# A program order for ACT and DVE in an attention stage, a second PSUM bank for its filler projections, paired statistics, and two start-up steps dealt otherwise

## The chip, the cores and the metric

The kernel runs on one core of a Trainium2 chip. The metric is the device time of one execution, in microseconds (us). The core's engines are TensorE (PE, its weight loads shown as PEld), VectorE (DVE), ScalarE (ACT), GpSimd (POOL) and SyncE (SP, which here issues nearly all DMAs). Each takes its instructions in one fixed order, and they meet through semaphores.

## The reference

One step of a hybrid encoder with one mixer layer, 1024 prompt frames and 32 running frames, width 1024, 16 heads of 64. Both branches read one normalized input:

```python
h = rmsnorm(x, norm_g)
q, k = rmsnorm(h @ Wq, q_g) * 64**-0.5, rmsnorm(h @ Wk, k_g)    # per head
v, logf = h @ Wv, log_sigmoid(h @ Wf + b_f)
ga, gb, ma, mb = h @ Wga, h @ Wgb, h @ Wma, h @ Wmb
u = (h @ Wua) * sigmoid(h @ Wub)
o = causal_softmax_attention(q, k, v, bias = C[t] - C[s])       # C = cumsum(logf)
conv = causal_depthwise_conv(u, w_dw, width 31) + b_dw
ya = (o * silu(ga)) @ w_pa
yb = (silu(layernorm(conv)) * silu(gb)) @ w_pb
y = x + (sigmoid(ma) * ya + sigmoid(mb) * yb) @ w_out
```

The 32 running frames attend to 512 cached keys besides their own. Outputs are y, k, v, logf and the last convolution rows, all fp32.

## The kernel before

**Products.** For accuracy each operand is split into a high and a low part. A product is three matmuls (high by high, low by high, high by low). In the input projections the parts are fp16; in the attention and behind it they are fp32 rows. A projection of 128 output channels is three chunks of 352 frames, each of eight steps of three matmuls (`steps`, `mms` at L183). Each step of three calls `beat`: a tick, the clock of the program. Small jobs hang on ticks: `later(n, fn)` emits work n ticks on, `prep` holds the preparation of the next weights, and `taps` and `chores` are DVE work (convolution taps at L368, above all) dealt out at a fixed rate per tick.

**Weights.** A batch is two keys (or one half-width value key). In `begin`, the batch now starting emits: `load` of the following batch at ticks 5 and 15, `stage` (a sum of squares on ACT, L117, with a small POOL cast, L120) at 3 and 13, `total` (a PE sum across partitions) at 25, `power` at 27, and `split` (ACT writes the high part, L138, DVE the low part, L141) from 29 on. A batch of two keys lasts 48 ticks. So a load is issued in one batch, and its squares are taken in the next.

**Stages in order of time.** The opening transposes and splits x in three column groups (`x_split`) while it makes the first two projections (`high(i, p)` and `low(i, p)` split slice p of their weights, `known(i)` finds their scale, `rooted` takes the roots of the rows' squares, `squares(t)` the squares of row block t). Then come the values (L760), the convolution inputs u, keys and queries (`qk`), the gate ga, the attention, and the output products.

**Keys and queries.** ACT squares each chunk (L865) and writes the high part (L866), POOL the low part `sql` (L869), PE sums over heads with two fp32 matmuls into a bank of `st` (L876, L877), ACT forms the inverse root (L879, L880), and DVE scales the chunk out of PSUM (L883). The chunk's PSUM bank, one of five, is held until then. The statistics come 11 ticks behind the square, chunk by chunk.

**Attention.** The sequence `seq` holds 16 heads of 8 blocks and four `Sample` items for the running frames. `start(seq[n + 3])` makes the scores of the block three places ahead: PE into one of two buffers of psS (two banks each), DVE adds the mask (L1097) and takes the maximum (L1099), ACT the exponential P (L1102), DVE a reciprocal (L1104), POOL scales P (L1105). `turn` transposes block n on PE (L1119) into banks of psT, from which ACT copies the first four parts and DVE the rest (L1122). `values`, once a head, multiplies the transposed P with V (L1138) into two psT banks; ACT and DVE add them into ot (L1142, L1143, L1145). Between these PE gets `fill`: ticks of 22 gate projections of no urgency, each chunk in the single bank of the pool `pq`, copied out by ACT (L932). PE and SP run in the order of the program there; the order of ACT, DVE and POOL is found by a scheduler that simulates time. In the stages before the attention PE, DVE and ACT are all in program order.

```python
    pe.enter_context(tc.manual_schedule(engines={E.PE, E.SP}))
    ...
    psS = pool("psS", 2, stack=p2, space=PS)
    psT = pool("psT", 3, stack=p2, space=PS)
```

The eight PSUM banks of the attention are thus four of psS, three of psT and one of pq.

Of the kernel before, what the change touches and what calls it, by code (L numbers as in the profile page):

```python
# [53 lines left out]
def build(tc, xT, xt, wv, wf, ckT, cv, clT, stT, vec, cst, yT, kT, vO, lfO, cpT, csT):  # L54
# [166 lines left out]
    def begin():  # L221

        if not plan:
            return
        b = plan.pop(0)
        after = plan[0] if plan else None
        t = pace["tick"]
        jobs = [(25, b.total), (27, b.power)]
        if b.n == 2:
            jobs += [(3, lambda: b.stage(0)), (13, lambda: b.stage(1))]  # L230
            for i, n in ((0, 29), (1, 39)):
                jobs.append((n, lambda i=i: b.split(i)))
                jobs += [(n + 1 + 2 * p, lambda i=i, p=p: b.rest(i, p)) for p in range(3)]
        else:
            jobs += [(3 + 10 * i, lambda i=i: b.stage(i)) for i in range(2)]
            jobs.append((29, lambda: split.__setitem__(b.keys[0], split_v(b.keys[0][1], b))))
        if after:
            jobs += [(5 + 10 * i, after.load) for i in range(after.n)]
        prep.extend((t + n, fn) for n, fn in sorted(jobs, key=lambda e: e[0]))
# [377 lines left out]
    scale(1, 1, True)  # L617
    scale(0, 1)
    known(0)
    high(0, 0)  # L620
    low(0, 0)
    steps_of = {}

    def rooted(t0, nt):
        steps_of[t0] = root(t0, nt)
# [12 lines left out]
    for f in range(8):  # L638
# [12 lines left out]
    b1 = plan.pop(0)  # L651
    b2 = plan[0]
    x_split(0, ws0, u0, {
        0: [lambda: top(1), lambda: squares(2, False)],
        1: [lambda: squares(3)],
        2: [lambda: high(0, 1), lambda: low(0, 1)],
        3: [lambda: total(2), lambda: squares(4, False)],
        4: [lambda: known(1), lambda: rooted(2, 3), lambda: high(1, 0), lambda: low(1, 0), lambda: high(0, 2)],
        5: [lambda: steps_of[2](), lambda: scale(2, 0), lambda: scale(3, 0, True), lambda: scale(4, 0), lambda: low(0, 2)],
        6: [lambda: scale(3, 1, True), lambda: scale(2, 1), lambda: high(1, 1), lambda: low(1, 1)],  # L660
        7: [lambda: scale(4, 1), lambda: high(1, 2), lambda: low(1, 2)]})
# [189 lines left out]

    pqk = ExitStack()
    tp = pool("tp", 2, stack=pqk, side="right")
    def qk(g, f):
        gv, dst, smp = (vec_t[:, V_KG:V_KG + 1], s_k, ks_t) if g == "k" else (qg8, s_q, qs_t)
        qn = tp.tile([128, TT], F32, name="qn", tag="qn")
        gi = tp.tile([128, 1], F32, name="gi", tag="gi")

        def ev(c, sl, ps, inv):
            if c == 0:  # L860
                nc.gpsimd.tensor_scalar(gi, inv, gv, 1.0, op0=ALU.mult, op1=ALU.mult)
            sqf = tp.tile([128, CH], F32, name="sqf", tag="sqf")
            sqh = tp.tile([128, CH], F32R, name="sqh", tag="sqh", bufs=3)
            sql = tp.tile([128, CH], F32R, name="sql", tag="sql", bufs=3)
            nc.scalar.activation(sqf, ps, AF.Square, scale=inv)  # L865
            nc.scalar.copy(sqh, sqf)  # L866

            def low():
                nc.gpsimd.tensor_sub(sql, sqf, f32(sqh))  # L869

            later(2, low)
            later(11, lambda: root(c, sl, ps, sqh, sql))

        def root(c, sl, ps, sqh, sql):
            pm = st.tile([128, 512], F32, name="pst", tag="st")
            nc.tensor.matmul(pm[:, :CH], bones, sqh, start=True, stop=False)  # L876
            nc.tensor.matmul(pm[:, :CH], bones, sql, start=False, stop=True)  # L877
            ri = tp.tile([128, CH], F32, name="ri", tag="ri")
            nc.scalar.activation(ri, pm[:, :CH], AF.Ln, bias=eps_t, scale=1.0 / HD)  # L879
            nc.scalar.activation(ri, ri, AF.Exp, scale=-0.5)  # L880

            def scaled():
                nc.vector.scalar_tensor_tensor(qn[:, sl], ps, gi, ri, op0=ALU.mult, op1=ALU.mult)  # L883
                later(6, lambda: out(c))

            later(4, scaled)

        def out(c):
            n = CH if c < 2 else T - 2 * CH
            o = slice(c * CH, c * CH + n)  # L890
            qh = tp.tile([128, CH], F32R, name="qh", tag="qh")
            ql = tp.tile([128, CH], F32R, name="ql", tag="ql")
            nc.scalar.copy(qh[:, :n], qn[:, o])  # L893
            nc.gpsimd.tensor_sub(ql[:, :n], qn[:, o], f32(qh[:, :n]))  # L894
            nc.sync.dma_start(dst[0, f * 128:(f + 1) * 128, o], f32(qh[:, :n]))
            nc.sync.dma_start(dst[1, f * 128:(f + 1) * 128, o], f32(ql[:, :n]))
            if c == 2:
                if g == "k":
                    nc.sync.dma_start(kT[f], qn)
                nc.gpsimd.tensor_scalar(smp[:, f, :], qn[:, T:TT], 1.0, 1.0, op0=ALU.mult, op1=ALU.mult)  # L900

        proj((g, f), X, XL, pj, ev)
# [80 lines left out]


    pe = ExitStack()
    pe.enter_context(tc.manual_schedule(engines={E.PE, E.SP}))
    pace["rate"], pace["credit"] = R_A, 0.0
    taps.extend(sums(7))
    psS = pool("psS", 2, stack=p2, space=PS)
    psT = pool("psT", 3, stack=p2, space=PS)  # L990
    totals.append((psT, "T"))
    ap = pool("ap", 2, stack=p2, side="right")

    def filler():

        for n in range(NFILL):
            yield from gate_steps(*fills.pop(0), pq)

    flow = filler()

# [4 lines left out]
    class Sample:  # L1005
# [15 lines left out]
        def scores(self):  # L1021
            g, kc, pf = self.g, self.kc, self.pf
            ps = psS.tile([128, 2, 512], F32, name="psS", tag="S")
            for j in range(4):
                rows = slice(64 * (j % 2), 64 * (j % 2) + 64)
                q = qs_t[rows, 2 * g + j // 2, :]
                nc.tensor.matmul(ps[32 * j:32 * j + 32, 0, :], q, kc[rows, j // 2, :], start=True, stop=True)
                nc.tensor.matmul(ps[32 * j:32 * j + 32, 1, :TS], q, ks_t[rows, 2 * g + j // 2, :],
                                 start=True, stop=True)
            nc.vector.scalar_tensor_tensor(pf[:, :PAST], ps[:, 0, :], cq[:, g:g + 1], pf[:, :PAST],  # L1030
                                           op0=ALU.add, op1=ALU.subtract)
            nc.vector.scalar_tensor_tensor(pf[:, PAST:], ps[:, 1, :TS], cq[:, g:g + 1], pf[:, PAST:],
                                           op0=ALU.add, op1=ALU.subtract)
            nc.vector.tensor_add(pf[:, PAST:], pf[:, PAST:], smask)
            nm = ap.tile([128, 3], F32, name="nm", tag="nm", bufs=6)
            nc.vector.tensor_reduce(nm[:, 0:1], pf, axis=AX.X, op=ALU.max, negate=True)
            nc.scalar.activation(pf, pf, AF.Exp, bias=nm[:, 0:1], accum_out=nm[:, 1:2])
            nc.vector.reciprocal(nm[:, 2:3], nm[:, 1:2])
            nc.vector.tensor_scalar(pf, pf, nm[:, 2:3], None, op0=ALU.mult)

# [36 lines left out]
    class Block:  # L1077
# [5 lines left out]
        def scores(self):  # L1083
# [13 lines left out]
            nc.vector.tensor_add(diag, diag, cmask)  # L1097
            nm = ap.tile([128, 3], F32, name="nm", tag="nm", bufs=6)
            nc.vector.tensor_reduce(nm[:, 0:1], ps[:, :nb, :w], axis=AX.XY, op=ALU.max, negate=True)  # L1099
            self.P = P = ap.tile([128, T], F32, name="P", tag="P", bufs=3)  # L1100
            with tc.issue_after(sides["tables"].ins):
                nc.scalar.activation(P[:, :nk].rearrange("p (b w) -> p b w", b=nb), ps[:, :nb, :w], AF.Exp,  # L1102
                                     bias=nm[:, 0:1], accum_out=nm[:, 1:2])
            nc.vector.reciprocal(nm[:, 2:3], nm[:, 1:2])  # L1104
            nc.gpsimd.tensor_scalar(P[:, :nk], P[:, :nk], nm[:, 2:3], 1.0, op0=ALU.mult, op1=ALU.mult)  # L1105

# [94 lines left out]
    sides["shift"] = ap.tile([128, TT], F32, name="shift", bufs=1)  # L1201
    nc.sync.dma_start(sides["shift"], s_m)
    heads[1].load()
    start(seq[0])
    fill(8)
    start(seq[1])
    fill(4)
    start(seq[2])
    for n, b in enumerate(seq):
        if n + 3 < len(seq):  # L1210
            start(seq[n + 3])
        if n + 9 < len(seq) and getattr(seq[n + 9], "i", 1) == 0:
            seq[n + 9].head.load()
        if n + 6 < len(seq) and isinstance(seq[n + 6], Sample):
            seq[n + 6].load()
        if getattr(b, "i", 0) == 3 and b.head.h + 1 < H:
            heads[b.head.h + 1].load_v()
        if isinstance(b, Sample):
            fill(4)
            b.turn()  # L1220
        else:
            b.turn()
            fill(4 if b.i > 2 or b.head.h != 8 else 0)
        if n >= 2 and pending(seq[n - 2]):
            seq[n - 2].values()
        if n >= 3 and isinstance(seq[n - 3], Sample):
            seq[n - 3].finish()
        if "ready" in sides:
            next(ln, None)
# [402 lines left out]
```

## Time and profile before

| | |
|---|---|
| median of three runs | 1370.6 us (1367.92 to 1372.93) |
| profiled execution | 1370.8 us |
| its span, first to last instruction | 1368.9 us |
| mean granted clock of TensorE | 0.993 |
| busy share of PE, DVE, ACT, POOL | 97%, 71%, 53%, 37% |

The profile is of one execution. "Busy" of an engine is the time in which one of its instructions ran. Matmuls overlap in the array, so PE is shown busy for longer than it takes to issue them. The profile notes for each instruction how long its engine had been idle before it and what released it; a wait for several things is put down to the one that came last. The "chain" follows the work back from the last instruction through what released each step.

### The profile page before, as it was taken

Reading aid. Unit: us, or ns where it says so; the run is one execution under the profiler, and the core shown is the slowest. Engines: PE = TensorE matmul, PEld = TensorE weight load, DVE = VectorE, ACT = ScalarE, POOL = GpSimd, SP = SyncE. Lnnn points to the kernel's source line nnn. Section 1 sums busy time; section 2 is a strip of 40 time slices with the busy share of each in tenths; the row PEclk is TensorE's granted clock in tenths of the full one; section 3 lists DMA queues with packets and bytes.
Section 4 is the critical chain, followed back from the end, with each engine's and each line's share of the span. In section 5 each row is a group of like instructions: output and inputs, shape, how many; then the busy total and the mean of one; then the engine's idle time right before and its main releaser. Section 6 shows DMA issues by size and latency. Waiting matters only on the chain.

```text
span 1368.9 us, 24793 instructions
## 1 busy us (share of the span) xinstructions
PE 1321.6 (97%) x9383; PEld 1004.6 (73%) x9383; DVE 976.6 (71%) x1534; ACT 721.7 (53%) x1360; POOL 500.2 (37%) x548
## 2 busy tenths in 40 slices
PE   8999999999999999989999899999999999999999
PEld 5577876666666666666667667667666699999998
DVE  6787879778888897978778756644454479266664
ACT  6544555757676743555545556655555466333320
POOL 2001125547475820244323232222222239355553
PEclk9999999999999999999999999999999999999999
DMA  6233233425252453544634644455542597634462
GB/s 246 96 129 109 91 111 120 132 88 176 94 172 78 172 160 110 162 106 130 168 108 125 173 124 123 130 158 126 144 118 80 177 327 261 212 114 141 145 194 68
DMA packets 113495, 194.96 MB, mean 142 GB/s; under 512 B 34080, under 2 KB 80032, under 8 KB 113376
## 3 DMA queue, kind: packets, MB, share of 16 engines
q1 hardware_dynamic: 113232, 193.31, 46.2%
q8 instruction: 74, 1.21, 0.4%
q14 instruction: 45, 0.37, 0.1%
q10 hardware_dynamic: 144, 0.07, 0.0%
HBM read 127.68 MB, written 65.64 MB: 141 GB/s over the span
## 4 chain that ended last, share of the span: by engine, by line
PE 73%; DVE 8%; DMA 6%; ACT 6%; issue 4%; SPq 1%; POOL 1%; ACTq 0%; DVEq 0%; POOLq 0%
PE pj L183 51%; PE pjv L760 6%; PE pj L1464 5%; DMA raw<-wf 4%; PE po L1138 3%; PE ptr L1119 2%; DVE y L368 2%; DVE nm L1099 2%; ACT P L1102 2%; PE psS L1094 1%; PE psS L1095 1%; DVE wl L141 1%; ACT t L932 1%; ACT junk L117 1%; DMA a<-s_o 1%
## 5 line engine op out<-in xcount | busy, mean ns | idle before, releaser
L183 PE MATMUL pj<-xh,wh 128*128 128x352 f16 (+2 forms) x1536 | 483.8, 315 | 20.9 <-ACT t L932 17.1
L183 PE MATMUL pj<-xh,wl 128*128 128x352 f16 (+2 forms) x1536 | 483.3, 315 | 0.4 <-DVE wl L141 0.4
L183 PE MATMUL pj<-xl,wh 128*128 128x352 f16 (+2 forms) x1536 | 483.2, 315 | 0.4 <-DVE xl L576 0.2
L183 PEld LDWEIGHTS <-wh 128*128 128x128 f16 x3072 | 302.2, 98 | 164.0 <-ACT wh L138 3.6
L368 DVE SCALAR_TENSOR_TENSOR y<-u,vec_t,y 128x1086 f32<-128x1086 f32 x240 | 343.7, 1433 | 9.5 <-ACT y L365 6.6
L1105 POOL TENSOR_SCALAR P<-P,nm 128x128 f32<-128x128 f32 (+7 forms) x128 | 122.1, 955 | 281.0 <-DVE nm L1104 231.2
L183 PEld LDWEIGHTS <-wl 128*128 128x128 f16 x1536 | 151.1, 98 | 93.7 <-issue 22.4
L141 DVE SCALAR_TENSOR_TENSOR wl<-raw,sc,wh 128x384 f16<-128x384 f32 (+1 forms) x192 | 120.8, 663 | 31.5 <-ACT wh L138 31.5
L1102 ACT ACTIVATE P<-psS,nm 128x128 f32<-128x128 f32 (+7 forms) x128 | 94.7, 740 | 77.9 <-DVE nm L1099 64.1
L1099 DVE TENSOR_REDUCE nm<-psS 128x1 f32<-128x128 f32 (+7 forms) x128 | 96.2, 754 | 7.1 <-DVE psS L1097 0.5
L1122 ACT COPY pt<-ptr 128x512 f32<-128x512 f32 (+3 forms) x128 | 64.2, 502 | 59.9 <-PE ptr L1119 59.0
L175 POOL TENSOR_TENSOR wl<-raw,wh 128x384 fp32r<-128x384 f32 (+1 forms) x51 | 63.3, 1268 | 75.0 <-ACT wh L172 57.8
L1094 PE MATMUL psS<-KB,QB 128*128 128x256 f32 (+2 forms) x192 | 81.9, 428 | 9.0 <-ACT P L1102 8.9
L117 ACT ACTIVATE junk<-raw 128x1024 bf16<-128x1024 f32 x62 | 65.2, 1052 | 37.8 <-DMA raw<-wf 37.7
L1119 PE MATMUL ptr<-ident,P 128*128 128x128 f32 x576 | 85.0, 274 | 0.0
L869 POOL TENSOR_TENSOR sql<-sqf,sqh 128x352 fp32r<-128x352 f32 x48 | 59.4, 1238 | 49.9 <-ACT sqh L866 49.8
L138 ACT ACTIVATE wh<-raw,sc 128x1024 f16<-128x1024 f32 (+1 forms) x68 | 72.6, 1089 | 6.8 <-DVE sc L158 6.6
L1119 PEld LDWEIGHTS ptr<-ident,P 128*128 128x128 f32 x576 | 69.8, 142 | 5.7 <-ACT pt L1122 0.2
L1138 PE MATMUL po<-pt,V 128*64 128x256 f32 x640 | 72.6, 382 | 0.0
L120 POOL CAST topb<-tops 128x2 bf16<-128x2 f32 x35 | 12.9, 367 | 162.8 <-ACT junk L117 112.8
L894 POOL TENSOR_TENSOR ql<-qn,qh 128x352 fp32r<-128x352 f32 (+1 forms) x48 | 62.8, 1311 | 22.2 <-ACT qh L893 22.2
L1097 DVE TENSOR_TENSOR psS<-psS,cmask 128x128 f32<-128x128 f32 x128 | 37.5, 294 | 46.8 <-PE psS L1095 46.2
(271 smaller groups left out, 2601.9 us busy)
## 6 DMA issues: line engine op xcount, KB each, us to landing
raw<-wf SPq DMA_DIRECT2D x92, 512.0 KB
QB<-s_q SPq DMA_DIRECT2D x32, 256.0 KB
KB<-s_k SPq DMA_DIRECT2D x32, 256.0 KB
kT<-qn SPq DMA_DIRECT2D x8, 528.0 KB
s_ga<-t SPq DMA_DIRECT2D x24, 176.0 KB
s_gb<-t SPq DMA_DIRECT2D x24, 176.0 KB
s_ma<-t SPq DMA_DIRECT2D x24, 176.0 KB
s_mb<-t SPq DMA_DIRECT2D x24, 176.0 KB
```

The costliest lines, as they stand in the source:

```text
L117: nc.scalar.activation(junk[:, :raw.shape[1] * raw.shape[2]], raw.rearrange("p a b -> p (a b)"), AF.Square, accum_out=self.tops[:, i:i + 1])
L138: nc.scalar.mul(wh[:, ks, :], raw[:, ks, :], self.s[:, i:i + 1])
L141: nc.vector.scalar_tensor_tensor(wl[:, ks, :], raw[:, ks, :], self.s[:, i:i + 1], wh[:, ks, :], op0=ALU.mult, op1=ALU.subtract)
L183: nc.tensor.matmul(ps, a[:, kt, :], b(kt, sl), start=(first and n == 0), stop=(last and n == N - 1))
L368: t = nc.vector.scalar_tensor_tensor(y, u[:, i:i + CW], w, y, op0=ALU.mult, op1=ALU.add)
L760: nc.tensor.matmul(ps[:, :VC], a, b, start=(n == 0), stop=(n == 23))
L1094: nc.tensor.matmul(ps[:, b, :wm], QB[:, qsl], KB[:, ksl], start=True, stop=False)
L1099: nc.vector.tensor_reduce(nm[:, 0:1], ps[:, :nb, :w], axis=AX.XY, op=ALU.max, negate=True)
L1102: nc.scalar.activation(P[:, :nk].rearrange("p (b w) -> p b w", b=nb), ps[:, :nb, :w], AF.Exp, bias=nm[:, 0:1], accum_out=nm[:, 1:2])
L1105: nc.gpsimd.tensor_scalar(P[:, :nk], P[:, :nk], nm[:, 2:3], 1.0, op0=ALU.mult, op1=ALU.mult)
L1119: nc.tensor.transpose(pt[:, 128 * j:128 * j + 128], P[:, 128 * (4 * u + j):128 * (4 * u + j) + 128], ident)
L1138: nc.tensor.matmul(po[rows], V[:, j, :], parts[c][:, j, :], start=(c % 2 == 0 and j < 2), stop=(c % 2 == 1 and j >= 2 * c))
```

## The change

- Attention: DVE and ACT join PE and SP in program order. psT has two banks for three, and the freed bank becomes a second pool `pq2`; the fills' chunks take `pq` and `pq2` in turn.
- The blocks' and samples' `scores` are cut in three: scores up to the maximum, `soft` (the exponential) and `norm` (reciprocal and scaling). In step n they are emitted as: scores of n+3, turn of n, soft of n+3, norm of n+2. The fill of four ticks is cut in two halves with the values between them.
- Keys and queries: the statistics of two chunks are made together, 13 ticks behind the second one's square; sqh and sql have four buffers for three.
- First value weights: stage at ticks 10 and 17 (from 3 and 13), total at 32 (from 25), power at 33 (from 27), split at 34 (from 29).
- Opening: the first slice of the first split moves behind the first transposes; `known(1)` and `squares(4)`, the latter from DVE to ACT, change places; the second split's first slice goes ahead of the roots.

```diff
         jobs = [(25, b.total), (27, b.power)]
-        if b.n == 2:
+        if b.keys[0] == ("v", 0):
+            jobs = [(32, b.total), (33, b.power), (10, lambda: b.stage(0)), (17, lambda: b.stage(1)),
+                    (34, lambda: split.__setitem__(b.keys[0], split_v(0, b)))]
+        elif b.n == 2:
...
     known(0)
-    high(0, 0)
-    low(0, 0)
...
     x_split(0, ws0, u0, {
-        0: [lambda: top(1), lambda: squares(2, False)],
+        0: [lambda: high(0, 0), lambda: low(0, 0), lambda: top(1), lambda: squares(2, False)],
...
-        3: [lambda: total(2), lambda: squares(4, False)],
-        4: [lambda: known(1), lambda: rooted(2, 3), lambda: high(1, 0), lambda: low(1, 0), lambda: high(0, 2)],
+        3: [lambda: total(2), lambda: known(1), lambda: squares(4)],
+        4: [lambda: high(1, 0), lambda: low(1, 0), lambda: rooted(2, 3), lambda: high(0, 2)],
...
+    duo = []
+
+    def stats(both):
+        pms = [st.tile([128, 512], F32, name="pst", tag="st") for _ in both]
+        for pm, (_, sqh, sql) in zip(pms, both):
+            nc.tensor.matmul(pm[:, :CH], bones, sqh, start=True, stop=False)
+            nc.tensor.matmul(pm[:, :CH], bones, sql, start=False, stop=True)
+        for i, (pm, (fn, _, _)) in enumerate(zip(pms, both)):
+            later(i, lambda pm=pm, fn=fn: fn(pm))
...
             later(2, low)
-            later(11, lambda: root(c, sl, ps, sqh, sql))
+            duo.append((lambda pm: root(c, sl, ps, pm), sqh, sql))
+            if len(duo) == 2:
+                both = list(duo)
+                duo.clear()
+                later(13, lambda: stats(both))
...
-    pe.enter_context(tc.manual_schedule(engines={E.PE, E.SP}))
+    pe.enter_context(tc.manual_schedule(engines={E.PE, E.SP, E.DVE, E.Activation}))
...
-    psT = pool("psT", 3, stack=p2, space=PS)
+    psT = pool("psT", 2, stack=p2, space=PS)
+    pq2 = pool("pq2", 1, stack=p2, space=PS)
...
+    class Two:
+        n = 0
+
+        def tile(self, *a, **k):
+            self.n += 1
+            return (pq2 if self.n % 2 else pq).tile(*a, **k)
...
-            yield from gate_steps(*fills.pop(0), pq)
+            yield from gate_steps(*fills.pop(0), two)
...
             nc.vector.tensor_reduce(nm[:, 0:1], ps[:, :nb, :w], axis=AX.XY, op=ALU.max, negate=True)
+            self.at = ps, nm, nk, nb, w
+
+        def soft(self):
+            ps, nm, nk, nb, w = self.at
             self.P = P = ap.tile([128, T], F32, name="P", tag="P", bufs=3)
...
+        def norm(self):
+            P, nm, nk = self.P, *self.at[1:3]
             nc.vector.reciprocal(nm[:, 2:3], nm[:, 1:2])
...
-        if isinstance(b, Sample):
-            fill(4)
-            b.turn()
-        else:
-            b.turn()
-            fill(4 if b.i > 2 or b.head.h != 8 else 0)
+        b.turn()
+        if n + 3 < len(seq):
+            seq[n + 3].soft()
+        if n + 2 < len(seq):
+            seq[n + 2].norm()
+        some = 2 if isinstance(b, Sample) or b.i > 2 or b.head.h != 8 else 0
+        fill(some)
         if n >= 2 and pending(seq[n - 2]):
             seq[n - 2].values()
+        fill(some)
```

More of the change, by code (lines that the diff above doesn't have):

```diff
@@ L862, in ev @@
             sqf = tp.tile([128, CH], F32, name="sqf", tag="sqf")
-            sqh = tp.tile([128, CH], F32R, name="sqh", tag="sqh", bufs=3)
-            sql = tp.tile([128, CH], F32R, name="sql", tag="sql", bufs=3)
+            sqh = tp.tile([128, CH], F32R, name="sqh", tag="sqh", bufs=4)
+            sql = tp.tile([128, CH], F32R, name="sql", tag="sql", bufs=4)
             nc.scalar.activation(sqf, ps, AF.Square, scale=inv)
@@ L871, in ev, with root @@
             later(2, low)
-            later(11, lambda: root(c, sl, ps, sqh, sql))
[L874 to L877, printed above, removed]
+            duo.append((lambda pm: root(c, sl, ps, pm), sqh, sql))
[3 more added lines that the diff above has]
+                later(13, lambda: stats(both))
+        def root(c, sl, ps, pm):
             ri = tp.tile([128, CH], F32, name="ri", tag="ri")
@@ L989, in build @@
     psS = pool("psS", 2, stack=p2, space=PS)
-    psT = pool("psT", 3, stack=p2, space=PS)
+    psT = pool("psT", 2, stack=p2, space=PS)
+    pq2 = pool("pq2", 1, stack=p2, space=PS)
     totals.append((psT, "T"))
     ap = pool("ap", 2, stack=p2, side="right")
+    class Two:
[3 more added lines that the diff above has]
+            return (pq2 if self.n % 2 else pq).tile(*a, **k)
+    two = Two()
     def filler():
         for n in range(NFILL):
-            yield from gate_steps(*fills.pop(0), pq)
+            yield from gate_steps(*fills.pop(0), two)
     flow = filler()
@@ L1034, in scores @@
             nc.vector.tensor_add(pf[:, PAST:], pf[:, PAST:], smask)
-            nm = ap.tile([128, 3], F32, name="nm", tag="nm", bufs=6)
+            self.nm = nm = ap.tile([128, 3], F32, name="nm", tag="nm", bufs=6)
             nc.vector.tensor_reduce(nm[:, 0:1], pf, axis=AX.X, op=ALU.max, negate=True)
-            nc.scalar.activation(pf, pf, AF.Exp, bias=nm[:, 0:1], accum_out=nm[:, 1:2])
+        def soft(self):
+            nc.scalar.activation(self.pf, self.pf, AF.Exp, bias=self.nm[:, 0:1], accum_out=self.nm[:, 1:2])
+        def norm(self):
+            nm, pf = self.nm, self.pf
             nc.vector.reciprocal(nm[:, 2:3], nm[:, 1:2])
@@ L1099, in scores, with soft @@
             nc.vector.tensor_reduce(nm[:, 0:1], ps[:, :nb, :w], axis=AX.XY, op=ALU.max, negate=True)
+            self.at = ps, nm, nk, nb, w
+        def soft(self):
+            ps, nm, nk, nb, w = self.at
             self.P = P = ap.tile([128, T], F32, name="P", tag="P", bufs=3)
@@ L1103, in scores, with norm @@
                                      bias=nm[:, 0:1], accum_out=nm[:, 1:2])
+        def norm(self):
+            P, nm, nk = self.P, *self.at[1:3]
             nc.vector.reciprocal(nm[:, 2:3], nm[:, 1:2])
@@ L1203, in build @@
     heads[1].load()
-    start(seq[0])
-    fill(8)
-    start(seq[1])
-    fill(4)
-    start(seq[2])
+    for n in range(3):
+        start(seq[n])
+        seq[n].soft()
+        if n:
+            seq[n - 1].norm()
+        fill((8, 4, 0)[n])
     for n, b in enumerate(seq):
@@ L1217, in build @@
             heads[b.head.h + 1].load_v()
-        if isinstance(b, Sample):
-            fill(4)
-            b.turn()
-        else:
-            b.turn()
-            fill(4 if b.i > 2 or b.head.h != 8 else 0)
+        b.turn()
[5 more added lines that the diff above has]
+        fill(some)
         if n >= 2 and pending(seq[n - 2]):
             seq[n - 2].values()
+        fill(some)
         if n >= 3 and isinstance(seq[n - 3], Sample):
```

## Prediction

> **What bounds the kernel now.** I read the page first (engine shares, chain, groups), then the table by stage, then PE's waits, then the timeline around the longest of them.
>
> ```profile
> span 1368.9 us, 24793 instructions
> PE 1321.6 (97%) x9383; PEld 1004.6 (73%) x9383; DVE 976.6 (71%) x1534; ACT 721.7 (53%) x1360; POOL 500.2 (37%) x548
> L183 PE MATMUL pj<-xh,wh 128*128 128x352 f16 (+2 forms) x1536 | 483.8, 315 | 20.9 <-ACT t L932 17.1
> 479.62 21.50 PE pj L183 x144
> ```
>
> PE is the bound: busy for 97% of the span. But each matmul lasts 315 ns, and 144 in a row take 21.50 us on the chain, one every 149 ns (a "tick", three of them, is 0.448 us). So an idle time shown for PE hides another 315 - 149 = 166 ns of lost issue. The question is where PE is not issuing. By stage (columns: window, length, busy time of PE, PEld, DVE, ACT, POOL with counts, PE's clock, DMA):
>
> ```profile
> 270.00:480.00 210.00, 205.82 (x1376) 135.94 (x1374) 175.53 (x208) 144.64 (x263) 128.61 (x115) 1.00 0.39 127
> 430.00:475.00 45.00, 45.00 (x303) 29.93 (x302) 39.92 (x45) 35.41 (x67) 35.03 (x29) 1.00 0.44 146
> 570.00:790.00 220.00, 205.01 (x1458) 146.86 (x1460) 171.16 (x317) 118.15 (x248) 75.63 (x93) 0.98 0.48 132
> 790.00:1076.00 286.00, 271.26 (x2042) 195.47 (x2035) 156.07 (x387) 156.74 (x344) 68.21 (x124) 0.99 0.45 124
> ```
>
> The last two rows are the attention, 506 us with 29.7 us of idle PE; the first is the key and query stage, where ACT and DVE already run in the kernel's order: 4.2 us idle in 210. PE's waits, who for whom, total, times, longest:
>
> ```profile
> PE pj L183 <- ACT t L932: 17.1, 19, 2.4
> PE psS L1094 <- ACT P L1102: 8.9, 6, 2.6
> PE pst L877 <- POOL sql L869: 5.0, 4, 1.8
> PE pj L183 <- ACT wh L138: 2.4, 1, 2.4
> PE tot L129 <- POOL topb L120: 2.0, 1, 2.0
> PE psn L1168 <- DVE ot L1143: 1.6, 1, 1.6
> PE psS L1027 <- ACT P L1102: 1.2, 1, 1.2
> ```
>
> Rows one, two, six and seven lie in the attention: a fill's next chunk finds its one bank not yet copied out by ACT (L932), or the scores find both banks of psS unread by the exponential (L1102). Why is ACT late? One case in full, and the sum of its kind in the attention:
>
> ```profile
> 903.54 0.58 SPq L109 DMA_DIRECT2D raw<-wf  x1
> 911.59 1.06 ACT L117 ACTIVATE junk<-raw 128x1024 bf16<-128x1024 f32 x1 [3.81 <-DMA raw<-wf]
> 912.65 0.53 ACT L932 ACTIVATE t<-pj,sc 128x352 f32<-128x352 f32 x1
> 913.23 0.45 PE L183 MATMUL pj<-xh,wh 128*128 128x352 f16 x1 [2.43 <-ACT t L932]
> ACT junk L117 <- DMA raw<-wf: 34.9, 14, 4.7
> ```
>
> The weights' sum of squares (L117) stands in ACT's queue right behind its load, 8 us after the issue, and ACT sits idle 3.81 us with PE's copy behind it. In the code the load is at tick 5 of one batch and the squares at tick 3 of the next, 46 ticks later. The scheduler, which orders ACT and DVE here, pulled the squares forward.
>
> **The clock.** PE's granted clock falls to half for 3.4 us behind long waits:
>
> ```profile
> 63.30:66.70 3.40, 3.40 (x14) 1.75 (x13) 2.01 (x5) 2.65 (x4) 0.26 (x1) 0.50 0.02 5
> 913.20:916.60 3.40, 3.37 (x13) 1.76 (x12) 0.00 (x0) 2.23 (x5) 0.18 (x1) 0.51 0.14 53
> 63.20 9.76 PE pj L183 x54
> 695.75 1.28 PE ptr L1119 x6
> 697.02 2.43 PE pj L183 x12
> 783.27 3.46 PE pj L183 x12
> 787.12 0.66 PE ptr L1119 x6
> 913.23 3.61 PE pj L183 x12
> ```
>
> Twelve fp16 matmuls take 12 x 0.149 = 1.79 us at full clock. Here they take 3.61 and 3.46, and at 695.75 six transposes and twelve matmuls take 0.62 and 0.64 too long: 1.82 + 1.67 + 1.26 = 4.8 us lost in the attention. At 63.20, 54 take 9.76 instead of 8.06: 1.7 us.
>
> The Trainium skill ("TensorE: Matmul & The Clock Gate", Part 1: The HAM clock gate) puts the half rate behind at least one idle window of about 3.4 us. This trace disagrees: the dips at 63.2 and 913.2 follow waits of 2.0 and 2.4 us. By that rule the dips are not the waits' and stay, and the sum would be 1342 for 1336.
>
> **The change, part by part.** The sum is made against the profiled execution, 1370.8 us; the median of the three runs is 1370.6.
>
> *1. Attention in the kernel's order, fills in two banks.* The squares go back to 46 ticks behind their load, so ACT meets landed data. The fills' copy-out of a chunk now has eight ticks and two blocks' other matmuls before its bank is wanted. The exponential of block n+3 is emitted behind the turn of block n, the reciprocal of n+2 one step later, when its exponential is done. Removed: idle 17.1 + 8.9 + 1.6 + 1.2 = 28.8 us; 27 waits with a hidden 0.166 each, 4.5; the dips, 4.8. Together 38.1 us.
>
> What comes back: in a fixed order a late head of the queue holds all behind it. DVE per step does mask and maximum of n+3, half the copies of n, a reciprocal, then taps; what is queued behind a maximum that waits for PE's scores is the copy that frees a psT bank, and psT has two banks for three. In the attention's first 220 us DVE is nearly full:
>
> ```profile
> L368 DVE SCALAR_TENSOR_TENSOR y<-u,vec_t,y 128x1086 f32<-128x1086 f32 x49 | 67.9, 1387 | 0.1
> L1099 DVE TENSOR_REDUCE nm<-psS 128x1 f32<-128x128 f32 (+7 forms) x56 | 41.9, 753 | 2.8
> SPq L1147 <- DVE ot L1145: 35.3, 5, 8.3
> ```
>
> DVE's 171.2 us there must fit into about 220 less the 15 us of idle less tails and dips, some 200: 85%. Bounds of the new waits: none (430 to 475, a program-ordered stretch at 89% DVE, has PE busy all 45.00 us), to 29, all the old ones in new places. I take the row 270 to 480, program order at 84% DVE: 4.2 / 210 = 2%, of 468 us 9.4. It is nearest in order and in load. The values now stand between two halves of a fill, 20 times (16 heads, 4 samples) one more change between fp32 and fp16 matmuls; between 0 and a tail of 0.166 each, I take 1.0 in all. On SP the values' issues (the store of ot, which waits for DVE up to 8.3 us) now stand ahead of two ticks of fill; queued behind are gate stores and weight loads. The loads run 46 ticks ahead, so nothing on the path: 0. POOL stays with the scheduler; its scaling of P gains nothing and has two steps, 0. Attention: -38.1 + 9.4 + 1.0 = **-27.7**.
>
> *2. First value weights.* Total from tick 25 to 32, squares from 3 and 13 to 10 and 17.
>
> ```profile
> 59.10 1.07 ACT L117 ACTIVATE junk<-vraw 128x1040 bf16<-128x1040 f32 x1 [4.50 <-DMA vraw<-wv]
> 61.81 1.14 POOL L120 CAST topb<-tops 128x2 bf16<-128x2 f32 x1 [20.20 <-ACT junk L117]
> ```
>
> The load still decides when the squares run, and topb is there at about 63. Seven ticks are 3.1 us, more than the wait of 2.0, so wait, tail and dip go: 2.0 + 0.17 + 1.7 = **-3.9**. The split starts at tick 34 and has 14 ticks (6.3 us) for two ACT scalings and four DVE halves; late by a little it would cost a microsecond of these.
>
> *3. Statistics for two chunks.* PE's four waits for sql stand before the 5th, 17th, 24th and 29th of 48 statistics; the 17th:
>
> ```profile
> 305.18 0.43 PE L877 MATMUL pst<-sql,bones 128*128 128x352 f32 x1 [1.63 <-POOL sql L869]
> 319.84 0.54 ACT L865 ACTIVATE sqf<-pj,sc 128x352 f32<-128x352 f32 x1
> 331.71 0.57 DVE L883 SCALAR_TENSOR_TENSOR qn<-pj,gi,ri 128x352 f32<-128x352 f32 x1
> 377.29 3.60 PE pj L183 x24
> 381.20 3.60 PE pj L183 x24
> ```
>
> Odd ones are first of a pair and get ten ticks (4.5 us) more: gone. The 24th gets two ticks, 0.9 us. Of 5.0 + 4 x 0.166 = 5.7 about 4.6 returns. But a pair's first chunk holds its bank ten ticks longer. There are five banks and a chunk each 3.91 us, so a bank is wanted 15.6 us after its last matmul. In the worst chunk the scaling ended 12.4 us after the square began; plus 4.5 is 16.9, late by 1.3. Bounds: 0, to 24 x 1.3 = 31 if all lagged so; few do, I take 2.0 (three or four of the 24, and something for the scaling queue). **-2.6**.
>
> *4. Opening.* high(0,0) and low(0,0) behind the first transposes, the second split's first slice ahead of the root, squares(4) on ACT.
>
> ```profile
> 17.98 0.28 PE L183 MATMUL pj<-xh,wh 128*128 128x256 f16 x1 [2.44 <-ACT wh L138]
> ```
>
> The most it can bring is this wait, its tail and one dip, 2.4 + 0.17 + 1.7 = 4.3; the most it can cost is the square that ACT takes over (1.06 like the one at 911.59, with 0.19 to read its sum), 1.25 late. The wait should halve, but the rows of x that the next chunk needs are scaled behind the same square: I take **-0.8**.
>
> Sum: -27.7 - 3.9 - 2.6 - 0.8 = -35.0; 1370.8 - 35.0 = **1336 us**.
>
> **The rivals.**
>
> *The waits come back elsewhere.* Two psT banks, DVE's copies behind the maxima, and P one step later: new waits near their bound, 29 minus 9.4 more, some 22 with a dip: 1358. For it: DVE at 85% in the first 220 us, and a tap of 1387 ns just ahead of a maximum. Against: 430 to 475 at 89%.
>
> *Slower.* DVE becomes the bound through psT: a turn of blocks 4 to 7 needs both banks, and the second is freed by a copy behind the next maximum and any tap. There are 64 such turns. Two taps and a maximum (2 x 1.39 + 0.75 = 3.5 us) against the fill of four ticks between two turns (1.8 us) leave 1.7 us a turn at worst. It decides from (35 + 4) / 64 = 0.6 us on every one; at 0.7 a turn, 45 us, the time is 1381. Against it: after 790 the taps are over, DVE is at 156.07 of 286 us, and more than half of the attention lies there.
>
> *Almost nothing comes back*, as from 430 to 475, and the opening pays in part: 1336 - 9.4 - 2 - 3.5 = 1321.
>
> *The clock dips stay.* If they are not the waits', 4.8 + 1.7 remain: 1342. Each begins where a long wait ends, so I hold it unlikely. The Trainium skill's rule above ("TensorE: Matmul & The Clock Gate") would give this case.
>
> *The change doesn't do what it says*: the loads themselves are late, and ACT still waits for raw. The second bank then covers the fills, but the 8.9 + 1.2 us for P with tails and a dip stay: 1348. Against: 8 us of landing and 46 ticks, some 40 us.
>
> **How the numbers follow.** Chances: forecast 0.62 (its own range 1324 to 1348), waits elsewhere 0.17, almost nothing back 0.10, slower 0.05, clock 0.03, loads 0.03. About 0.3%, 4 us, is what a measurement here can tell from no change. Low end 1319: no new waits, no bank waits, nothing for the changes of type, the opening's 4.3 (38.1 + 3.9 + 4.6 + 4.3 = 50.9 off 1370.8, rounded down). High end 1358: the waits elsewhere. Slower 0.05 is its rival; of the waits elsewhere, a price near a bound, I give 0.03 to an end within 4 us; faster 0.92 is the rest.
>
> **What would show it.** Right: in the attention no PE wait for ACT t, no ACT junk waiting for raw, idle PE near 10 us, no row at clock 0.5 after 50 us; no wait for topb at 63; one wait for sql at most. Wrong: PE's transposes waiting for the copies of pt (psT), scores waiting for P behind a DVE maximum, or PE waiting for qn's bank between 217 and 475. The prediction fails most likely in the 9.4 us of new waits, the one term that no row of this trace shows directly.

## The result, and the profile after

The changed kernel takes 1349.27 us (1345.89 to 1353.69, four runs) against 1371.76 us of the kernel before on the same chip (1367.92 to 1374.4). The ratio is 0.9844, 95% interval [0.9818, 0.987], a gain of some 22 us. 1336 was forecast, a gain of 35. The profiled execution of the changed kernel is the quickest of its four, 1345.89, so it shows 24.9 us of gain.

The page of the changed kernel, with the lines that answer to those shown of before:

```profile
span 1344.1 us, 24837 instructions
PE 1312.6 (98%) x9383; PEld 1003.1 (75%) x9383; DVE 990.4 (74%) x1532; ACT 719.0 (53%) x1362; POOL 505.8 (38%) x548
L183 PE MATMUL pj<-xh,wh 128*128 128x352 f16 (+2 forms) x1536 | 481.6, 314 | 2.3 <-ACT wh L138 1.4
L1153 PE MATMUL ptr<-ident,P 128*128 128x128 f32 x576 | 88.6, 276 | 17.3 <-DVE pt L1156 9.2
```

The idle time ahead of the projections (L183) fell from 20.9 us to 2.3. But the transposes of P (L1153, which was L1119) now wait 17.3 us. Their row of before:

```profile
L1119 PE MATMUL ptr<-ident,P 128*128 128x128 f32 x576 | 85.0, 274 | 0.0
```

The table by stage (the columns of the tables before):

```profile
270.00:480.00 210.00, 209.17 (x1404) 139.74 (x1403) 191.22 (x214) 143.69 (x263) 127.10 (x116) 1.00 0.42 137
566.00:790.00 224.00, 210.47 (x1540) 151.24 (x1539) 175.72 (x333) 123.82 (x267) 87.75 (x101) 1.00 0.50 136
790.00:1052.30 262.30, 254.69 (x1919) 185.02 (x1917) 148.45 (x364) 150.71 (x328) 66.79 (x116) 0.99 0.46 126
```

The last two rows are the attention: 486.3 us for 506 in the rows of before, with 21.1 us of idle PE for 29.7. PE's waits in it (who for whom, total, times, longest), and then two of ACT's and DVE's:

```profile
PE ptr L1153 <- DVE pt L1156: 9.2, 11, 1.7
PE ptr L1153 <- ACT pt L1156: 6.4, 5, 2.2
PE po L1172 <- ACT pts L1078: 1.7, 2, 0.9
PE ptr L1153 <- DVE ot L1177: 1.2, 1, 1.2
PE po L1172 <- ACT mean L1211: 0.7, 1, 0.7
PE psS L1121 <- ACT P L1133: 0.6, 2, 0.4
...
ACT P L1133 <- DVE nm L1138: 70.9, 62, 3.1
ACT P L1133 <- DVE nm L1126: 38.4, 30, 3.3
DVE wl L141 <- ACT wh L138: 32.5, 20, 2.2
```

The old waits are gone: no PE wait for the fill's copy, 0.6 us for P, and no ACT sum of squares waiting for its load. In their place PE waits for the copies of the transposed P (L1156), 16 times, 15.6 us: it wants a bank of psT that has not been copied out.

Stage times from the two traces, each from PE's first instruction of the stage to that of the next (first projection of 352 frames, first value product, first scores, last product of P with V, end of the span):

| us | before | after | shown | forecast |
|---|---|---|---|---|
| opening | 49.64 | 49.19 | -0.45 | -0.8 |
| to the first value product | 26.51 | 22.64 | -3.87 | -3.9 |
| values, u, keys and queries, ga | 499.52 | 494.05 | -5.47 | -2.6 |
| attention | 500.55 | 486.37 | -14.18 | -27.7 |
| output products | 292.71 | 291.83 | -0.88 | 0 |

So 13.5 us of the forecast are missing in the attention, and some 3 us are gained beyond it elsewhere.

**What makes the copies late.** The longest of these waits, followed back along the chain of the changed kernel (start, length, what):

```profile
829.28 0.22 DVE psS L1124
829.50 0.03 issue
829.53 0.02 DVEq L1126
829.55 0.04 issue
829.60 1.09 DVE nm L1126
...
831.69 0.19 ACT P L1133
831.88 1.04 ACT wh L138
832.91 0.44 ACT t L944
833.36 0.38 ACT t L1215
833.74 0.48 ACT pt L1156
834.23 0.04 issue
834.27 0.33 PE ptr L1153
```
```profile
830.78 1.01 ACT L1133 ACTIVATE P<-psS,nm 128x896 f32<-128x896 f32 x1 [2.26 <-DVE nm L1138]
```

Mask and maximum on DVE are followed by the exponential on ACT (L1133), which had been idle 2.26 us for the maximum (second fence, from ACT's timeline; the bracket is the idle time and what ended it). In ACT's queue behind it stand a scaling of weights, the copy of a fill and a square of the layer norm, and only then the copy that PE waits for; DVE's low part of the weights waits on the same scaling. The exponential of block n+3 is emitted right behind the turn of n, so ACT comes to it before DVE has the maximum, and all behind it waits too: the two rows of ACT's waits for nm together are 109 us. (They name the reciprocal L1138 or the maximum L1126, whichever ended last; the maximum is what the exponential needs.)

### The profile page after: what moved, and what is told of

It reads as the page before. It is cut to its first block, busy times and chain, and to the rows that moved or that the text cites. A ratio compares the mean times of both kernels' runs of the same rounds, so it can differ in the third digit from the quotient of the medians.

```text
span 1344.1 us, 24837 instructions
## 1 busy us (share of the span) xinstructions
PE 1312.6 (98%) x9383; PEld 1003.1 (75%) x9383; DVE 990.4 (74%) x1532; ACT 719.0 (53%) x1362; POOL 505.8 (38%) x548
## 4 chain that ended last, share of the span: by engine, by line
PE 82%; DVE 9%; ACT 3%; issue 2%; DMA 2%; SPq 1%; POOL 0%; DVEq 0%; ACTq 0%; POOLq 0%
PE pj L183 56%; PE pjv L761 6%; PE pj L1501 6%; PE po L1172 4%; PE ptr L1153 3%; DVE nm L1126 2%; DVE wl L141 2%; DVE y L371 2%; PE psS L1122 2%; PE psS L1121 2%; DMA ga<-s_ga 2%; ACT wh L138 1%; DVE psS L1124 1%; DMA s_q<-qh 1%; PE warm L477 1%
## 5 line engine op out<-in xcount | busy, mean ns | idle before, releaser
L183 PE MATMUL pj<-xh,wh 128*128 128x352 f16 (+2 forms) x1536 | 481.6, 314 | 2.3 <-ACT wh L138 1.4
L183 PE MATMUL pj<-xh,wl 128*128 128x352 f16 (+2 forms) x1536 | 481.2, 313 | 0.7 <-DVE wl L141 0.6
L183 PE MATMUL pj<-xl,wh 128*128 128x352 f16 (+2 forms) x1536 | 480.9, 313 | 0.5 <-DVE xl L579 0.4
L183 PEld LDWEIGHTS <-wh 128*128 128x128 f16 x3072 | 301.5, 98 | 162.1 <-issue 7.1
L1139 POOL TENSOR_SCALAR P<-P,nm 128x128 f32<-128x128 f32 (+7 forms) x128 | 129.9, 1015 | 279.9 <-DVE nm L1138 229.8
L183 PEld LDWEIGHTS <-wl 128*128 128x128 f16 x1536 | 150.5, 98 | 72.0 <-DVE wl L141 1.6
L141 DVE SCALAR_TENSOR_TENSOR wl<-raw,sc,wh 128x384 f16<-128x384 f32 (+1 forms) x192 | 128.2, 693 | 48.3 <-ACT wh L138 48.3
L1133 ACT ACTIVATE P<-psS,nm 128x128 f32<-128x128 f32 (+7 forms) x128 | 95.1, 743 | 113.3 <-DVE nm L1138 70.9
L1126 DVE TENSOR_REDUCE nm<-psS 128x1 f32<-128x128 f32 (+7 forms) x128 | 97.0, 758 | 12.5
L1153 PE MATMUL ptr<-ident,P 128*128 128x128 f32 x576 | 88.6, 276 | 17.3 <-DVE pt L1156 9.2
L175 POOL TENSOR_TENSOR wl<-raw,wh 128x384 fp32r<-128x384 f32 (+1 forms) x51 | 63.3, 1270 | 74.3 <-ACT wh L172 58.6
L1153 PEld LDWEIGHTS ptr<-ident,P 128*128 128x128 f32 x576 | 69.2, 141 | 28.2 <-DVE pt L1156 12.1
L1156 ACT COPY pt<-ptr 128x512 f32<-128x512 f32 (+3 forms) x128 | 64.3, 502 | 44.4 <-PE ptr L1153 43.2
L906 POOL TENSOR_TENSOR ql<-qn,qh 128x352 fp32r<-128x352 f32 (+1 forms) x48 | 67.8, 1429 | 6.6 <-ACT qh L905 6.5
L761 PE MATMUL pjv<-vwh,xh 128*128 128x260 f16 x256 | 70.1, 274 | 0.0
L761 PE MATMUL pjv<-vwl,xh 128*128 128x260 f16 x256 | 70.0, 273 | 0.0
```

Source lines behind the costliest of these rows:

```text
L141: nc.vector.scalar_tensor_tensor(wl[:, ks, :], raw[:, ks, :], self.s[:, i:i + 1], wh[:, ks, :], op0=ALU.mult, op1=ALU.subtract)
L183: nc.tensor.matmul(ps, a[:, kt, :], b(kt, sl), start=(first and n == 0), stop=(last and n == N - 1))
L761: nc.tensor.matmul(ps[:, :VC], a, b, start=(n == 0), stop=(n == 23))
L1153: nc.tensor.transpose(pt[:, 128 * j:128 * j + 128], P[:, 128 * (4 * u + j):128 * (4 * u + j) + 128], ident)
```

## The experiments

The theory after the result: the order did what it should for the squares, and its price is this queue: the exponential, emitted early, holds the fill's copies and the copies of the next turn behind it. Rivals: the gain came from the second fill bank and not from the order; psT has a bank too few; DVE waits for the gate ga and is late itself.

**Order by the scheduler again, banks and cut fills kept.**

```diff
-    pe.enter_context(tc.manual_schedule(engines={E.PE, E.SP, E.DVE, E.Activation}))
+    pe.enter_context(tc.manual_schedule(engines={E.PE, E.SP}))
```

> The changed kernel, with ACT and DVE in the attention ordered by the scheduler again; two fill banks, two psT banks and the cut fills stay. Order theory: the scheduler pulls the squares forward to their loads again, ACT idles 25 us or more on raw in the attention, PE's waits for P come back with about 10 us, the second fill bank hides the copies of t: 1360 us (10 to 15 more than the changed kernel). Bank theory (the second fill bank did it all, the order only added waits of the queue): no later than 1349, PE's waits for pt under 5 us.

1361.39 us, ratio to before 0.9949 [0.9931, 0.9966]. ACT waits 44.7 us in 17 for its loads again, and the attention takes 503.59 us (before: 500.55). What is left of the gain comes from the earlier stages. The second bank without the order brings the attention nothing.

**The order alone: one fill bank, three for the turns** (the cut scores and fills stay).

```diff
-    psT = pool("psT", 2, stack=p2, space=PS)
-    pq2 = pool("pq2", 1, stack=p2, space=PS)
+    psT = pool("psT", 3, stack=p2, space=PS)
...
-            return (pq2 if self.n % 2 else pq).tile(*a, **k)
+            return pq.tile(*a, **k)
```

> The changed kernel with three psT banks and one fill bank, as before the change; program order stays. Theory of the two psT banks: PE's waits for pt fall from 15.6 us to under 4, and its waits for ACT t come back, 5 to 17 us, since ACT's copy of a chunk stands behind an exponential that waits for DVE: 1343 to 1360. If ACT is punctual in program order, waits for t stay under 4 us and the time falls to 1335. If DVE and ACT are just too full, the waits move and the time stays at 1349.

1369.09 us, 0.9996 [0.9986, 1.0006]: no gain, and beyond my range. PE's waits in the attention, in this kernel (its line numbers are one smaller from L1003 on):

```profile
PE pj L183 <- ACT t L944: 36.4, 35, 4.0
PE psn L1201 <- DVE ot L1176: 1.7, 1, 1.7
PE ptr L1152 <- POOL P L1138: 0.9, 1, 0.9
```

The copies of pt no longer delay PE, so psT did want the third bank; but now the fill's copy does, for twice as long as before the change (17.1). ACT's timeline ahead of one such wait (1.59 us, ended at 592.01), with its idle time in brackets:

```profile
589.27 1.11 ACT L1132 ACTIVATE P<-psS,nm 128x1024 f32<-128x1024 f32 x1 [1.02 <-DVE nm L1125]
590.28 0.19 ACT L1132 ACTIVATION_READ_ACCUMULATOR P<-psS,nm 128x1 f32 x1
590.38 1.14 ACT L138 ACTIVATE wh<-raw,sc 128x1024 f16<-128x1024 f32 x1
591.42 0.54 ACT L944 ACTIVATE t<-pj,sc 128x352 f32<-128x352 f32 x1
```

It is the same queue with another victim. In the attention the order alone costs 9 us (509.48), the second bank alone 3 (503.59), and both together gain 14.

**Turn first, then the scores.** If the copy of a turn is late because it stands behind the exponential of the same step, the turn can go ahead of the scores.

```diff
+        b.turn()
         if n + 3 < len(seq):
             start(seq[n + 3])
...
-        b.turn()
```

> The changed kernel with the turn of block n emitted ahead of the scores of block n+3, so that DVE's and ACT's copies out of psT no longer stand behind the maximum and the exponential of n+3. Queue theory: PE's waits for DVE pt fall from 9.2 us to under 3, those for ACT pt from 6.4 to under 4, with no new wait for P over 3: 1340 us. Load theory (DVE at 85% in the first half, whatever the order): as much comes back at P or at the scores: 1349 within 3.

1364.43 us, 0.9962 [0.9949, 0.9975], 15 us slower than the changed kernel. PE waits 14.4 us in 9 for ACT's pt, up to 4.4, and 4.4 us in 6 for POOL's P. ACT's idle time for the maximum rises from 109 to 161 us. The turn of a step is now closer to the exponential of the step before it, with only the fill of four ticks (1.8 us) between. The theory was wrong in this form: what holds a copy is the exponential of the step before and what was queued behind that.

**The gate loaded earlier** (at block 1 of a head, not block 5).

```diff
-            if self.i == 5 and self.head.h % 2:
+            if self.i == 1 and self.head.h % 2:
```

> The changed kernel with the gate rows ga of an odd head loaded at its block 1 and not at block 5. DVE's idle time for ga (9.9 us, six times) falls to under 1. If these stops of DVE's queue hold the copies out of psT back, PE's waits for pt fall by 3 to 5 us and the time to 1345. If DVE makes them good while PE does the values, the time stays at 1349 within 2.

1346.27 us, 0.9835 [0.9816, 0.9855]; the changed kernel has 0.9844 [0.9818, 0.987]. DVE's wait for ga (9.9 us in 6) has left the list, but PE's waits for pt are still 10.4 and 6.7 us. DVE's wait for the gate is not the cause.

**The changed kernel again**, on the chip of the next three.

> The changed kernel itself, once more, beside the next kernels on their chip: 1346 to 1350 us, its attention 486 us long, 15 to 20 us of PE's waits for the copies out of psT.

1349.75 us, 0.9859 [0.9835, 0.9883]. The attention takes 489.51 us here, 3.1 more than in the first profile: that much differs from one execution to another, and the attention's gain is 11 to 14 us. The difference shows in PE's rows: its waits in the attention are 22.7 us for 20.4, the longest 3.46 for 2.20, and behind that longest wait PE works at the half clock for longer than in the first profile's one dip (5.48 us for 3.40):

```profile
834.12 0.47 PE L1153 MATMUL ptr<-ident,P 128*128 128x128 f32 x1 [3.46 <-ACT pt L1156]
834.12:839.60 5.48, 5.48 (x21) 3.80 (x22) 3.92 (x11) 1.96 (x5) 1.52 (x1) 0.50 0.09 33
```

**The exponential later in the step: between the values and the second half of the fill.**

```diff
         b.turn()
-        if n + 3 < len(seq):
-            seq[n + 3].soft()
...
             seq[n - 2].values()
+        if n + 3 < len(seq):
+            seq[n + 3].soft()
         fill(some)
```

> The changed kernel with the exponential of block n+3 (soft) emitted behind the first half of the fill, not in front of it. Queue theory, in the form that the turn-first kernel left: a copy out of psT stands in ACT's queue behind the exponential of the step before, which waits for DVE's maximum, and behind the weight scaling and the fill's copy that stand behind that. Then ACT's idle time before the exponentials (109 us in the attention) falls by half, as the fill's work goes first, PE's waits for ACT pt fall from 6.4 us to under 3 and those for DVE pt by a third, since DVE's wl waits less for ACT wh (32 us): 6 to 10 us off, 1340. Load theory: waits move to P, time within 3 of the changed kernel.

1343.03 us, 0.9809 [0.9793, 0.9825]. ACT's waits for the maximum fall from 109 to 87 us (56.8 + 30.4), DVE's for the high weights from 32.5 to 19.0, PE's for pt from 15.6 to 8.6; a wait for POOL's P of 3.0 is new.

**The exponential at the end of the step, behind both halves of the fill and the values** (the same two lines, behind the second `fill(some)`).

> The same with the exponential at the end of the step, behind both halves of the fill and the values. Queue theory: ACT's idle time before the exponentials nearly gone, but the exponential now runs while PE makes the next scores, so copies of the next turn stand right behind it (up to 1.1 us) and the scores two steps on may wait for P: waits for ACT pt 4 to 8 us, for P up to 4, time 1340 to 1350, not better than the exponential in the middle. Load theory: 1349.

1334.18 us, 0.9744 [0.9726, 0.9762]: 15 us under the changed kernel, where I had not expected the last place to beat the middle one. Waits of PE, ACT and DVE in the attention:

```profile
PE ptr L1153 <- DVE pt L1156: 5.2, 7, 1.8
PE ptr L1153 <- ACT pt L1156: 2.7, 2, 2.0
...
ACT P L1133 <- DVE nm L1138: 23.8, 28, 2.2
ACT P L1133 <- DVE nm L1126: 13.1, 14, 2.0
DVE wl L141 <- ACT wh L138: 10.0, 13, 1.8
```

All waits of this chain fall together: ACT's for the maximum to 37 us, DVE's behind it to 10, PE's for pt to 7.9. The attention takes 472.72 us, 13.7 less than in the changed kernel's first profile, with no other edit. Of these, 9.9 are idle time of PE (11.3 us for 21.1) and up to 1.7 the dip of the clock that this execution lacks. This is the main evidence for the theory, though it had not foreseen the size.

**The statistics chunk by chunk again** (one chunk at a time, 11 ticks behind its square), one run.

```diff
-            if len(duo) == 2:
+            if len(duo) == 1:
...
-                later(13, lambda: stats(both))
+                later(11, lambda: stats(both))
```

> The changed kernel with the statistics made chunk by chunk again, 11 ticks behind the square. If the paired statistics are what shortened the key and query stage (first value product to first score 494.05 us in the changed kernel, 499.52 before), this stage takes 499.5 again, with PE's waits for sql back at 5 us. If part of the gain is POOL's order elsewhere, it takes 496 to 498.

1353.9 us. The stage of keys and queries is back at 499.39 us, with its four waits; the same window in the changed kernel has one wait in all, for a bank. First row this kernel, second the changed one:

```profile
PE pst L861 <- POOL sql L880: 5.0, 4, 1.8
```
```profile
PE pj L183 <- DVE qn L895: 0.8, 1, 0.8
```

**Exponential last, gate early** (both edits above).

> The kernel with the exponential at the end of the step, and the gates ga loaded at block 1 of a head instead of block 5. By the queue theory (the copies of pt were late because the exponential stood ahead of them, not because DVE waited for ga) nothing more is gained: 1331 to 1337, as the one with the exponential last (1334). By the rival, that with the exponential out of the way DVE's waits for ga (9.9 us in the changed kernel) are what still delays DVE's copies of pt (5.2 us of PE's waits there), some 5 us go: 1327 to 1330, and the row of PE's transposes waiting for DVE's pt falls under 2 us.

1330.76 us (1328.78 to 1336.88), 0.9737 [0.972, 0.9754]. PE's wait for DVE's pt is 3.0 us, the attention 469.52. The interval lies across that of the exponential last alone: if the gate brings anything, it is a few microseconds, and this stays open.

**Exponential last, with one fill bank and three for the turns** (the edit of the order alone and that of the exponential last).

> The exponential at the end of the step, with one fill bank and three banks for the turns (as in the kernel before) instead of two and two. PE's waits for the fill's copy were 36.4 us in 35 when the exponential stood ahead of that copy in ACT's queue. If the queue was the cause, the copy is now ahead of the exponential, the waits fall under 10 us, and the time is 1338 to 1348. If the second bank itself is what counts (a chunk's copy-out takes half a microsecond however early it is issued, and the next chunk wants the bank at once), 20 us or more of them stay and the time is 1352 to 1365.

1331.52 us, 0.9725 [0.9712, 0.9738]. The row of the fill's copy, 36.4 us above:

```profile
PE pj L183 <- ACT t L944: 3.0, 8, 0.6
PE psS L1048 <- ACT P L1132: 2.8, 1, 2.8
```

One emission moved takes 33 of 36 us of waits away, and the second fill bank is not needed: the attention takes 473.54 us with three and one, 472.72 with two and two. The bank had only covered for copies that stood behind the exponential. The Trainium skill ("Perfetto Trace Analysis", Optimizing Tensor Performance, Matmuls) advises to rotate independent groups through different banks, so that one's copy-out overlaps the next one's matmuls. These runs agree where the copies are late (1369.09 with one fill bank, 1349.27 with two) and show no gain from it where they are early (1331.52 and 1334.18). The three versions with the exponential last in program order are the quickest here, and their intervals overlap.

**The exponential one turn later still** (of block n+2, behind the turn of n; reciprocal and scaling at the end of that step).

```diff
         b.turn()
-        if n + 3 < len(seq):
-            seq[n + 3].soft()
-        if n + 2 < len(seq):
-            seq[n + 2].norm()
+        if 0 < n < len(seq) - 2:
+            seq[n + 2].soft()
...
         fill(some)
+        if n + 2 < len(seq):
+            seq[n + 2].norm()
```

> The exponential of a block one turn later still: that of block n+2 behind the turn of block n, its reciprocal and the scaling of P at the end of the same step. ACT's wait for the maximum (70 and 40 us in the changed kernel, 24 and 13 with the exponential at the end of the step) goes under 10 us. If that wait in ACT's queue is all that delays the copies of pt, the time falls again, to 1326 to 1331. If the margin is now used up on the other side, the exponential stands ahead of the fill's copy again and P is ready only a step before its turn: waits of PE for P (psS's banks, or POOL's scaled P) of 5 to 15 us appear, and the time is 1336 to 1350. I hold the second likelier.

1337.2 us, 0.9767 [0.9753, 0.978], 5.7 us above the previous kernel on the same chip, and 3.0 above the one with the exponential last and the same banks (1334.18, on another chip; their intervals overlap a little). ACT's longest row for the maximum is down to 2.1 us, so that wait is not all that counts. The margin is used up on the other side:

```profile
PE ptr L1153 <- POOL P L1139: 4.8, 6, 2.3
PE ptr L1153 <- ACT pt L1156: 2.0, 3, 0.7
```

P is scaled too late for its turn. The attention is 6.2 us longer than with the exponential last, though PE's listed waits are no longer in sum; two stretches at a lower clock (0.54 from 647.6 to 651.0 us, 0.64 from 817.6 to 821.0) are part of it, the rest is not accounted for.

**Exponential last, order by the scheduler again.**

> ACT and DVE ordered by the scheduler again, as in the kernel before, with two fill banks and two for the turns, and the exponential emitted at the end of the step. Against the kernel with the exponential last (1334 and 1331) this undoes only the order. If the order is still needed when the exponential comes last, the squares are pulled forward onto loads still under way (17 waits of ACT for raw, 44.7 us, in the scheduler's version with the exponential behind the turn) and the time is 1352 to 1362. If the place of the exponential was all that counted, the scheduler's version comes to 1330 to 1338 too. I hold the first likelier, since the loads and squares are not moved by this edit.

1362.43 us, 0.9959 [0.9941, 0.9976]. Moving the exponential does nothing under the scheduler's order (1361.39 behind the turn):

```profile
PE psS L1121 <- ACT P L1133: 7.6, 7, 1.8
PE ptr L1153 <- DVE ot L1177: 5.0, 4, 3.0
PE ptr L1153 <- ACT pt L1156: 4.7, 9, 0.9
...
ACT junk L117 <- DMA raw<-wf: 44.5, 17, 5.3
```

The squares are again pulled onto loads under way. So the fixed order is needed, and the exponential's place decides what that order costs. That the squares alone make the scheduler's version slower is argued from their 44.5 us of ACT's idle time; no run moves them by themselves. All together, in us (fill banks and turn banks in brackets; the first is the kernel before, which lacks the other parts too; in the company of these runs it took 1367.91 to 1371.76):

| | exponential early | exponential last |
|---|---|---|
| scheduler (1, 3) | 1371.76 | not run |
| scheduler (2, 2) | 1361.39 | 1362.43 |
| program order (1, 3) | 1369.09 | 1331.52 |
| program order (2, 2) | 1349.27 | 1334.18 |

## Why the prediction was right in sign and 13 us short in size

*First value weights, right.* -3.87 for -3.9. The wait for topb is gone, and the stretch behind it is at full clock, as forecast: PE makes 27 matmuls there for 14. It is 22.64 us in every kernel that has this part; no run undoes it alone.

*Paired statistics, right in mechanism, undersized.* -5.47 for -2.6, confirmed by undoing it (+5.34). All four waits went, not 4.6 of 5.7 us; and the new bank waits, put at 2.0 between bounds of 0 and 31, came out at 0.8, once.

*Opening, not resolved.* -0.45 for -0.8. Over the kernels with this part the opening is 49.1 to 50.6 us. The wait for wh fell from 2.4 to 1.4 us, as forecast. What came instead is not rows of x that are late: PE's transposes of x wait 1.8 us (0.5 before) for the bank that DVE reads in making the low part of x, and ahead of the first of these reads in DVE's queue stand two scalings of rows of x and a low part of weights (19.26 to 21.41 us):

```profile
PE ptx L576 <- DVE xl L579: 1.8, 2, 1.3
PE pj L183 <- ACT wh L138: 1.4, 2, 0.8
```

*What goes in the attention, right.* The squares meet landed data, the fill's copies and P are in time. Undoing the order brings the waits for loads back (44.7 us).

*The clock, mostly right.* Of the four dips quoted behind the opening none is left; the row of 63.3 us is at 1.00 now. One new one is in the attention of the changed kernel's first profile, and it costs up to half of 3.4 us (another place in the second, shown above):

```profile
63.30:66.70 3.40, 3.40 (x27) 2.22 (x26) 2.13 (x6) 2.02 (x2) 0.27 (x1) 1.00 0.00 0
825.50:828.90 3.40, 3.40 (x14) 2.37 (x13) 1.86 (x5) 1.85 (x4) 0.80 (x1) 0.50 0.67 159
```

It stands behind two waits of 1.25 and 0.57 us, which ended 2.0 and 0.9 us before it. The Trainium skill's rule ("TensorE: Matmul & The Clock Gate", Part 1: The HAM clock gate) puts the half rate behind an idle window of some 3.4 us. The wait of 3.46 us in the second profile fits it; the other dips, behind waits of 1.25 to 2.6 us, don't, and the old ones went with their waits. What does set them is open: with the exponential last there are waits of 1.8 and 2.0 us and no dip behind the opening.

*The step that failed: "I take the row 270 to 480, program order at 84% DVE: 4.2 / 210 = 2%, of 468 us 9.4. It is nearest in order and in load."* The changed kernel has 21.1 us of idle PE in the attention, and over 20 waits with their hidden 0.166 us each, some 3.5 more, which I had not put on the new waits. Together that is 24 for 9.4. The prediction had named this term as the likeliest to fail, and the first of its signs of being wrong, transposes that wait for the copies of pt, is there. The row itself was the wrong one: PE's waits in that window of the kernel before are a single kind,

```profile
PE pst L877 <- POOL sql L869: 4.2, 3, 1.8
```

the very waits that the paired statistics were to remove. In the changed kernel the window has 0.8 us of idle PE at 91% DVE (191.22 of 210): how full DVE is says little here about what an order costs; what stands in the queue behind a late instruction does. The row that bore on it was in the trace of before and I did not use it, ACT's idle time ahead of the exponentials:

```profile
ACT P L1102 <- DVE nm L1099: 64.1, 60, 2.8
```

Where a scheduler orders ACT, what is ready can be emitted into such gaps; in an order written out everything behind the exponential stands still with it, and in the changed kernel the gaps are 109 us. I named the copy behind "a maximum that waits for PE's scores" on DVE; the exponential that waits for that maximum on ACT, with the fill's copy and the weights behind it, I left out. The rival of waits that come back elsewhere (1358) had the victim, psT, and the size nearly right (29 for 24), but DVE's load as its cause; the kernel with the exponential last has DVE as busy (994.0 us for 990.4) and half of these waits.

The total missed by less than the attention did, because the other stages gained some 3 us more than forecast; that the two errors have opposite signs is luck. The rival of late loads gave 1348, the number nearest to the result, and that is chance too: no sum of squares waits for its load in the changed kernel. What no run separates is the 1.0 us put on the values between two halves of a fill.

## What to carry to other kernels

Before fixing the order of two engines, list on each queue the instruction that waits longest for another engine, and what stands behind it: here that, and not the engine's load, set the price of the order. Then emit the waiting instruction as late as its consumer allows, behind the copies that others need: in this kernel one moved emission was worth 15 us and made a second PSUM bank needless, and moving it one step further cost 3 to 6 us again. Two parts that each lose alone (in the attention the order costs 9 us, the bank 3) can gain together (14), since the one covers for the other's cost.

## What was not expected of the hardware

The half clock can follow waits far shorter than its own length, and no single wait decides it. Half clock for 3.4 us came behind idle times of 1.25 and 0.57 us in the changed kernel, and behind 2.02 us in the kernel before; full clock came behind the changed kernel's longest wait in the same execution, 2.20 us, and behind 2.46 us in the kernel before (at 607.04 us). So the price of a wait of some 2 us differs by up to 1.7 us from one place to another. It can be more: behind the 3.46 us of the changed kernel's second profile, 5.48 us of PE's work ran at half clock, up to 2.7 us lost. With 2.3 us more of waits, this makes up about the 3.1 us between its two profiles.
